# Softmax products for two heads at once, and a spread through DRAM in place of a matmul, in a hybrid decoder layer

## The chip, the core and the metric

The kernel runs on one core of a Trainium2 chip. The metric is the device time of one execution in microseconds. A core has five engines that each work through a queue of their own in order: TensorE (PE in the profile; its weight loads stand apart as PEld), VectorE (DVE), ScalarE (ACT), GpSimd (POOL) and SyncE (SP), which issues the DMA transfers. They meet through semaphores: an instruction waits for what it needs, and all behind it on its engine wait too.

## What is computed

One decoder layer for a sequence of 512 tokens of width 1024, in float32. A combined input projection feeds two mixers side by side, sparse attention (8 heads of 64) and gated DeltaNet (4 heads of 128); their outputs are projected, gated and merged, then normalised; a gated MLP with a short convolution follows, and a second normalisation. Cut to what the change touches:

```python
def reference(x, ...):
    ...
    y_a = nsa_attention(...) @ w_nsa_out        # three branches: compressed, selected, sliding window
    y_b = gated_deltanet(...) @ w_gdn_out
    mix = (sigmoid(gate_a) * y_a + sigmoid(gate_b) * y_b) @ w_o
    x = layer_norm(ALPHA * x + mix, ...)
    return layer_norm(ALPHA * x + conv_ffn(x, ...), ...)

# in nsa_attention, for the selected (s) and the window (w) branch, causal:
    p = softmax(where(dist >= 0, q @ k.T * scale - slope * dist, NEG))
    o = g[1] * (p_s @ v_s) + g[2] * (p_w @ v_w) + g[0] * o_cmp

# in gated_deltanet, for each chunk of 64 tokens:
    m = where(strict, (k * beta) @ k.T * decay, 0)
    T = triangular_solve(eye + m, eye, lower=True, unit_diagonal=True)

def conv_ffn(x, w_up, conv_w, w_down):
    h = causal_dwconv(x @ w_up, conv_w)
    gate, val = split(h, 2)
    return (silu(gate) * val) @ w_down
```

## The kernel before

A product in float32 precision is made of float32r matmuls: each operand is split into a high part (a copy on ACT, `wh`, `dh`, `pth`) and a low part (a subtraction on DVE or POOL, `wl`, `dl`, `ptl`), and high times high, high times low and low times high are added up in PSUM. Small products are taken in float32 as they are; such a matmul stands in the trace as two records.

The work has stages. The **first stage** (about 324 us) holds the input projection (31 of its 40 units of 128 columns, tile `pg`, three raw weight buffers `raw`), both mixers, and their small chains. Its order is written by hand: the code of each step (`q0`, `k0`, `i0`, `n0`, ...) is recorded by `draw`, engine by engine, and the table `GIVEN` then issues single instructions in one long list (`n0V` is the next DVE instruction of step `n0`). `PLACE` says which buffer each tile takes. Then come the merge (`pm`, `px`), the output projection (`pw`), the FFN's up products (`pu`, 22 units of two halves) and its down products (`pdna`, `pdnb`), which use a 2x2 block scheme with seven products: sums of blocks (`s1` to `s4`) are formed on DVE while the up products run. In those later stages a scheduler orders the instructions by the order of the code.

Three places matter here. **`gdn_tri`** (step `n`, one for each of the 4 DeltaNet heads) inverts the triangular matrix from diagonal blocks of 16 rows upwards. `f16` holds each row's 16 entries within its diagonal block, (128 rows, 4, 16). For the substitution each row needs the rows of its whole block, `lx`; to spread them, `f16` is multiplied with a mask and a matmul with `same` (ones where two rows share a block) sums over the partitions, in two parts of 512 and 256 columns, which ACT copies to `lx`. Then 15 pairs of small DVE operations follow (`ts<-lx,ts` and `ts<-ts,ts`), and products that join the blocks.

**`scores` and `flip`** (steps `s` and `f`, by head and unit) make the softmax of one or two blocks of 128 query rows, transpose it on PE, and split it into `pth` and `ptl`. After every second flip the products with the values (`vcat`) add into `po`, one bank for one head at a time; a causal block of two query tiles is multiplied whole, with a quarter that is zero:

```python
for br, _ in parts:
    for k in range(4 if t > 1 else 2):
        ...
        for i, src in enumerate((pth, ptl)):
            PE.matmul(o, w, src[:, br, b:b + 2, :], start=(u == 1 and k == 0 and i == 0), stop=False)
```

**The FFN loop** forms, at each odd unit, the sums `s1`, `s2` (with its split `hs`, `ls`) and `s4` for its block, in the profile `s<-fth`, `s<-s,fth`, `ls<-s,hs` and `s<-fth,s`; behind the first down product six adds (`x<-x,pdna`) empty its two banks, ahead of the second product `s2`.

Of the kernel before, what the change touches and what calls it, by code (L numbers as in the profile page):

```python
# [33 lines left out]
          ("same", 128), ("low", 128), ("m16", 128),  # L34
# [9 lines left out]
def shape_consts():  # L44
# [8 lines left out]
    c["same"] = p // 16 == j // 16  # L53
# [16 lines left out]
def layout(a):  # L70
# [18 lines left out]
    for i in range(8):  # L89
# [35 lines left out]
DRAWN = "q0 k0 i0 q1 j0 m0 c n0 i1 v0 j1 p0 v1 a0 o0 b0 y0 a1 b1 m1 n1 i2 j2 a2 b2 o1 y1 m2 v2 q2 a3 n2 b3 o2 y2 q3 p1 g0 k1 a4 i3 j3 b4 g1 m3 a5 n3 b5 a6 v3 g2 o3 b6 g3 a7 g4 b7 y3 g5 g6".split()  # L125
GIVEN = """
t0S@2 t0S@1 t0V@2 t0A@1 t0P@6 t0V@3 t0P@7 t0V@1 t0P@8 t0P@9 t0P@10 t0S t0A t0P@3 t0P@4 t0P@11 t0V t0P*3 t0S*2 t0V*2
t0A t0V t0P t0P@15 t0P@16 t0P@21 t0P*4 t2S t2A t0P@22 t0P@23 t2S t2A t0P*3 t2P@6 t2V*2 t2S t2A@3 t2A t2V t2P@3 t2P@9
t2P t2P@10 t2P@11 t2P*6 t2P@18 t2P@15 t2P@21 t2P@19 t2P@22 t2P*2 t2V t2P t2P@20 t2P@23 t2P*2 t4S@1 t4A@2 t4V@2 t4S
t4A@1 t4V@1 t4A t4P@9 t4P@10 t4V t4P t4P@3 t4P*2 t4S t4A t4P@11 t4P@6 t4P@7 t4P@21 t4P@8 t4P@22 t4P t4P@12 t4P@13 t4V  # L130
t4P@18 t4P t4P@15 t4P@16 t4P@17 t4P@19 t4P@20 t4P*2 t6S t6A t6S*2 t6A@2 t6A t6P@9 t6P@3 t6P@6 t6P t6V@2 t6V@1 t6P@10
t6P@7 t6V t6A t6P@4 t6P t6P@11 t6V t6P@8 t6P@18 t6P@5 t6P@19 t6P@20 t6P*5 t6P@21 t6P*4 w20S uA@8 w20A w20V w20A uA@2
uA@11 cV@8 cV@10 uA@5 w20V zS@6 dV@2 q0P*12 dV@3 dA*2 dV@4 dV@5 dV@6 dV@7 dV@8 dV@9 dV@1 dV@10 dV@11 q0P*12 w18S
w18A@1 w18V@1 uA@6 uV@2 zS@2 w21S w18A w18V k0P*15 dV@12 dV@13 dV@14 dV@15 k0P*2 uA@4 uA@7 uA@3 uA w0S q0A@2 q0A*2
dV@16 k0P*4 dV@17 dV@18 w0A zV@1 k0P q0V@2 q0V@1 q0V k0P w16S w0A w0V@1 w0V k0P k0V*4 dV@19 cS@1 i0P*13 zS@5 w21A w21V
dV@20 k0A*2 w1S uA@9 cV i0P*4 w1G i0P*3 s01P k0V*2 s01P i0P*3 s00P i0P q1P w21A q1P*12 s00P uV w1V i0V*2 dV@21 dV@22
w21V i0V zS s01V s01A q1P*8 uV@3 q1P*3 uA@10 zS i0V i0A zV w17S w1G dV@23 w1V dV@24 uV s04P*2 q1A uA j0P uV dA j0P*3
dV@25 dV@26 dV@27 dV j0P*12 w16A q1A@2 w16G q1A q1V@1 q1V@2 w16A w16G j0P*5 w4S j0P*3 q1V j0A w17A m0G j0V cP*19 i0G
cP m0P j0V*2 cS@3 m1V m0G m0P m0A cS i0G cP*4 dP w17V i0P dP i0P w4V w4V@2 dP i0P w4V*2 cA dA i0P j0A j0V i0A cS i0A
i1P*12 i0A*2 i0V@9 i0V cA*3 s01V m0P*4 n0V@2 m0P@8 i1P s00V s00A cP*2 m0V@1 dV m0P w17A w17V i0G s00V*2 i0V i1P i0V  # L140
m0P m0V s02P m0V m0P cP m0V@4 n0G i0V@8 m1G m0V@5 s04V*2 m0V i1P w2S n0V cP*21 cA*4 cV n0V w2V*2 n0P i1P w2V n0G n0P
w2V n0A i1P*4 n0A n0V s01V i1P*2 n0V*14 w5S i1P*2 cP*15 i1A i1V n0V*2 i0V n0V*2 f00P*2 j0P*3 f00P zS n0V j0P n0V*2
s04A@1 i1V w5A w5V n0V j0A*4 cP cV*2 i1V cA n1V@3 cA f00A s02P s02V s02A cV*3 i1A n0V*2 w7S v0P*18 n0V zS n0V v0P s03P
v0P s04A i1V n0V*2 s03P n0V*2 w5A s03V w3S cA cV w5V j1P v0P*4 v0A*2 j1P*10 cV n0P*2 s02V n0P*6 n0V n0A cP*3 cA*2
cA@15 f00V n0P*4 v0V n0V p0P*4 n0P@18 n0P@19 v0G j0V n0P@20 n0P@21 n0P@22 n0P@23 n0P@24 n0P@25 cV n0A@4 n0V@37 n0P*4
p0P n0A n0V p0P v0V p0P*2 s03A w6S w6A p0V*2 n0P*8 j1P*2 cA@16 cV n0A j1P*8 n0V p0V v0A j1P*2 cA@17 j1P s04V v1P w6A
j1A n0P@38 n0P@39 n0P@40 n0P@41 n0P*3 n0A@7 n0P f01P*3 n0A f01P s03V w3A v0V p0A@1 p0A*2 v0P*2 m3G v0P*2 w6V f01A j0G
v0A s04V cV n0P cA s03V cA y0V@1 n0P*3 n0V v1P*10 v0A*3 j1V*3 cA cV w6V p0A f01V s12P*2 s12V o0P w3A o0A w3G@1 i1P
i1A@6 i1P*3 i1A v1P*2 i1A v1P o0P s04V v1P w3G v1P*3 i1A s10P*2 s10V i1A s11P s12A cA f01P cV cA f01P i1A j1A v1P*3
# [96 lines left out]
def body(ctx: ExitStack, tc: tile.TileContext, d, out):  # L246
# [719 lines left out]
    def flip(h, u, s):  # L966
# [26 lines left out]
        if u < 5:  # L993
            return
# [443 lines left out]
```

## Time and profile before

| | us |
|---|---|
| median of 3 runs | 820.7 (820.41 to 820.8) |
| profiled execution | 821.42 |
| its span, first to last instruction | 819.6 |
| PE busy | 808.5 |
| DVE busy | 638.2 |
| ACT busy | 400.9 |
| POOL busy | 147.6 |

The span is the time between the first and the last instruction on the core; the profiled execution's own time is 1.8 us longer. Busy time counts an instruction from start to end; matmuls overlap, so PE's busy time tells that it always had work, not that it worked at its peak. Rows of groups have the line, engine, operation, out<-in by tile names, shapes and count, then the busy time in us and the mean duration of one in ns, then the idle time ahead of them. L1044 is the loop that issues the hand-written order, L261 the call that all recorded operations of the later stages pass through, so tile names tell more than lines. Rows of waits have who waited, for whom, the total in us, how often, and the longest. Timeline rows have the start and the duration in us. DMA rows have the number of transfers, the size of each, and the median time from issue to landing.

### The profile page before, as it was taken

The numbers are of one execution on the slowest core, as the hardware profiler recorded it, in microseconds if no ns is written. First come the engines' busy times: TensorE is split into PE (matmuls) and PEld (weight loads), VectorE is DVE, ScalarE is ACT, GpSimd is POOL, SyncE is SP. The second block draws the span as 40 slices with busy tenths as digits, with TensorE's granted clock in tenths as the row PEclk, the third lists the DMA queues.
The fourth block names the chain that finished last, engine by engine and source line by source line (L and its number), as shares of the span: only waits on it lengthen the run. The fifth ranks groups of instructions, "written<-read, shape, count | busy, mean of one in ns | idle before, by whom it ended". The sixth has DMA issues, their size and how long they took to land.

```text
span 819.6 us, 12072 instructions
## 1 busy us (share of the span) xinstructions
PE 808.5 (99%) x4244; PEld 684.8 (84%) x4244; DVE 638.2 (78%) x1379; ACT 400.9 (49%) x915; POOL 147.6 (18%) x127
## 2 busy tenths in 40 slices
PE   9999999999999999999999999999999999999996
PEld 9888888888888888887888897888888888878885
DVE  5979888887788777675467548878898889898767
ACT  5444665666776674534342023444444444566530
POOL 0031314232244401212300002111111011100001
PEclk9999999999999999999999999999999999999998
DMA  7432211111120201354463207555556655676922
GB/s 239 128 120 83 63 41 52 52 53 52 33 72 27 78 26 53 116 166 134 149 232 103 77 10 233 191 192 179 184 196 204 206 205 182 187 235 196 339 82 102
DMA packets 40252, 108.06 MB, mean 132 GB/s; under 512 B 4608, under 2 KB 5760, under 8 KB 39936
## 3 DMA queue, kind: packets, MB, share of 16 engines
q1 hardware_dynamic: 40192, 107.30, 39.7%
q8 instruction: 33, 0.54, 0.3%
q14 instruction: 27, 0.22, 0.1%
HBM read 93.65 MB, written 13.63 MB: 131 GB/s over the span
## 4 chain that ended last, share of the span: by engine, by line
PE 85%; DVE 6%; DMA 3%; ACT 2%; issue 2%; POOL 1%; SPq 0%; DVEq 0%; ACTq 0%; POOLq 0%
PE pu L261 25%; PE pg L1044 20%; PE pd L1044 8%; PE pa L1044 6%; PE pdna L261 5%; PE pdnb L261 5%; PE pm L261 5%; PE pw L261 3%; PE px L261 3%; PE po L1044 3%; PE pg L261 2%; DVE fa L261 1%; DVE x L261 1%; DVE wl L261 1%; DMA raw<-tdn 1%
## 5 line engine op out<-in xcount | busy, mean ns | idle before, releaser
L261 PE MATMUL pu<-mh,wl 128*128 128x512 f32 (+1 forms) x384 | 142.7, 372 | 0.7 <-DVE wl L261 0.7
L261 PE MATMUL pu<-mh,wh 128*128 128x512 f32 (+1 forms) x384 | 142.7, 372 | 0.0
L261 PE MATMUL pu<-ml,wh 128*128 128x512 f32 (+1 forms) x384 | 142.6, 371 | 0.0
L261 ACT ACTIVATE wh<-raw 128x512 fp32r<-128x512 f32 (+1 forms) x112 | 71.7, 643 | 80.7 <-PE pu L261 54.0
L261 DVE TENSOR_TENSOR wl<-raw,wh 128x512 fp32r<-128x512 f32 (+1 forms) x108 | 87.7, 817 | 25.6 <-ACT wh L261 21.6
L1044 PE MATMUL pg<-xh,wl 128*128 128x512 f32 x248 | 99.0, 402 | 0.0
L1044 PE MATMUL pg<-xl,wh 128*128 128x512 f32 x248 | 98.9, 400 | 0.0
L1044 PE MATMUL pg<-xh,wh 128*128 128x512 f32 x248 | 97.4, 399 | 0.0
L261 PEld LDWEIGHTS pu<-mh,wl 128*128 128x128 f32 x384 | 72.3, 188 | 13.6 <-DVE wl L261 1.2
L261 PEld LDWEIGHTS pu<-ml,wh 128*128 128x128 f32 x384 | 72.3, 188 | 12.6
L261 PEld LDWEIGHTS pu<-mh,wh 128*128 128x128 f32 x384 | 72.3, 188 | 12.4
L261 DVE SCALAR_TENSOR_TENSOR fa<-pu,fcw,fa 128x511 f32<-128x511 f32 x88 | 65.6, 746 | 10.0 <-ACT fa L261 8.6
L261 POOL TENSOR_TENSOR fth<-fth,fa 128x512 f32<-128x512 f32 x22 | 32.6, 1483 | 211.5 <-DVE fa L261 194.0
L1044 ACT ACTIVATE big<-big,mn 128x256 f32<-128x256 f32 (+3 forms) x84 | 46.0, 553 | 23.9 <-DVE mn L1044 22.2
L1044 POOL TENSOR_TENSOR wl<-raw,wh 128x512 fp32r<-128x512 f32 x28 | 36.6, 1313 | 99.7 <-ACT wh L1044 58.9
L1044 PEld LDWEIGHTS pg<-xh,wl 128*128 128x128 f32 x248 | 46.6, 188 | 9.5 <-issue 0.5
L1044 PEld LDWEIGHTS pg<-xl,wh 128*128 128x128 f32 x248 | 46.6, 188 | 9.0 <-issue 0.2
L1044 PEld LDWEIGHTS pg<-xh,wh 128*128 128x128 f32 x248 | 46.7, 188 | 8.7 <-issue 0.7
L261 ACT ACTIVATE dh<-raw 128x512 fp32r<-128x512 f32 x62 | 36.9, 624 | 23.9 <-DMA raw<-tdn 9.9
L261 DVE TENSOR_TENSOR dl<-raw,dh 128x512 fp32r<-128x512 f32 x62 | 41.1, 695 | 8.9 <-ACT dh L261 8.7
L1044 ACT ACTIVATE wh<-raw 128x512 fp32r<-128x512 f32 (+1 forms) x54 | 32.5, 607 | 9.1 <-PE pg L1044 5.0
L261 POOL TENSOR_TENSOR rs<-rs,minus_half 128x1 f32<-128x1 f32 x8 | 7.5, 942 | 163.2 <-DVE rs L261 163.2
(318 smaller groups left out, 1868.2 us busy)
## 6 DMA issues: line engine op xcount, KB each, us to landing
raw<-in_up SPq DMA_DIRECT2D x44, 512.0 KB, 4.0
raw<-in_wT SPq DMA_DIRECT2D x40, 512.0 KB, 3.5
traw<-in_down SPq DMA_DIRECT2D x22, 512.0 KB, 5.2
tdn<-traw SPq DMA_DIRECT2D x44, 256.0 KB, 2.7
raw<-tdn SPq DMA_DIRECT2D x20, 512.0 KB, 4.4
raw<-in_down SPq DMA_DIRECT2D x15, 512.0 KB, 4.0
raw<-in_wm SPq DMA_DIRECT2D x8, 512.0 KB, 3.6
raw<-in_wo SPq DMA_DIRECT2D x8, 512.0 KB, 3.5
```

The costliest lines, as they stand in the source:

```text
L261: return give(*a, **kw)
L1044: give(*a, **kw)
```

## The change

`gdn_tri` no longer uses `same`. `f16` is written to DRAM sixteen times by one DMA, and a second DMA reads, for each partition, the sixteen rows of its block from its own copy into `lx`, whose layout is now (16, 4, 16). The two masked multiplications, the two matmuls and the two copies of each head go.

```diff
+    f16d = tc.dram_tile([GH, 16, 128 * TT * 16], F32, name="f16d")
...
-        lx = R["lx"].tile((128, TT, 16, 16))
-        for r0, n in ((8, 16), (0, 8)):
-            rs = slice(r0, r0 + 8)
-            sh = (128, TT, 8, n)
-            gx = R["big"].tile(sh)
-            E(f"gx{n}", h).tensor_tensor(gx, bc(f16[:, :, None, :n], sh), bc(C["row"][:, None, rs, None], sh), op=OP.mult)
-            pl = dps(sh)
-            PE.matmul(pl, C["same"], gx, start=True, stop=True)
-            copy(E(f"lx{n}", h, "A"), lx[:, :, rs, :n], pl)
+        lx = R["lx"].tile((128, 16, TT, 16))
+        d = f16d[h]
+        SP.dma_start(out=bass.AP(tensor=f16d.tensor, offset=d.offset, ap=[[64, 128], [8192, 16], [1, 64]]),
+                     in_=bc(f16.rearrange("p c j -> p (c j)")[:, None, :], (128, 16, 64)))
+        SP.dma_start(out=lx.rearrange("p r c j -> p (r c j)"),
+                     in_=bass.AP(tensor=f16d.tensor, offset=d.offset, ap=[[1024, 8], [8192, 16], [1, 1024]]))
...
-            V.tensor_tensor(tmp[:, :, :n], lx[:, :, r + 1:, r], bc(xs[:, :, r:r + 1], (128, TT, n)), op=OP.mult)
+            V.tensor_tensor(tmp[:, :, :n], lx[:, r + 1:, :, r].rearrange("p r c -> p c r"),
+                            bc(xs[:, :, r:r + 1], (128, TT, n)), op=OP.mult)
```

In `flip`, the transposed softmax of two heads of a pair goes into one tile pair `pt` (high and low), and one matmul takes both heads. The block on the diagonal (`k == t`) is multiplied only where it is not zero. `po` now holds one half of the queries for two heads. Units are drawn for both heads of a pair, two at a time.

```diff
-        if t % 2 == 0:
+        pr, hh, e = h // 2, h % 2, u // 2
+        if (pr, e) not in PT:
+            PT[pr, e] = [R["pt"].tile((128, 2, 2, 4, 128), F32R) for _ in range(2)]
...
+        if t % 2 == 0 or hh == 0:
             return
...
+        split = [x.rearrange("p h b k c -> p h (b k c)") for x in PT.pop((pr, e))]
         for br, _ in parts:
-            for k in range(4 if t > 1 else 2):
...
+            for k in range(t + 1):
                 w = vcat[:, k, br, g].rearrange("p a b -> p (a b)")
-                for i, src in enumerate((pth, ptl)):
-                    PE.matmul(o, w, src[:, br, b:b + 2, :], start=(u == 1 and k == 0 and i == 0), stop=False)
+                a, z = (128 if k == t else 0), 256 * k + (0 if late else 512 * br)
+                for i, src in enumerate(split):
+                    PE.matmul(pout[:, :, a:], w, src[:, :, z + a:z + 256],
+                              start=(e != 1 and br == 0 and k == 0 and i == 0), stop=False)
...
         for i in range(2):
-            PE.matmul(pout, vcb[:, g, j].rearrange("p a b -> p (a b)"), PC[g][i], start=False, stop=(i == 1))
+            for n, pc in enumerate(PC[g]):
+                PE.matmul(pout[:, i], vcb[:, g, (h - 1 + i) % 4].rearrange("p a b -> p (a b)"), pc[:, ts],
+                          start=False, stop=(i == n == 1))
```

On PE, before, one such group in the middle of the first stage (`po` is the output bank, `pc` the compressed branch's probabilities; one pth and one ptl row of four equal pairs are shown with what follows):

```order
L1044 MATMUL po_182<-pth,vcat 128x256
L1044 MATMUL po_182<-ptl,vcat 128x256
L1044 MATMUL po_182<-pc_154,vcb 128x512
L1044 MATMUL pd_178<-sq_120,big_87 128x128
L1044 MATMUL pd_177<-kq_118 128x256
L1044 MATMUL po_182<-pc_155,vcb 128x512
```

And after, the end of a group for the later query tiles of two heads (`pg` is the input projection, which stands between):

```order
L1042 MATMUL po_184<-pt_156,vcat 128x512
L1042 MATMUL po_184<-pt_157,vcat 128x512
L1042 MATMUL po_184<-pt_156,vcat 128x2x128
L1042 MATMUL po_184<-pt_157,vcat 128x2x128
L1042 MATMUL pg_186<-xh,wl_166 128x512
L1042 MATMUL pg_186<-xh,wh_161 128x512
L1042 MATMUL po_184<-pc_154,vcb 128x256
L1042 MATMUL po_184<-pc_155,vcb 128x256
```

Products with the values now have 512 columns, or twice 128 on the diagonal; those with `vcb` have 256 and are twice as many. In the whole program 192 + 16 `po` matmuls become 96 + 32.

The first stage's order (`GIVEN`, `DRAWN`, `PLACE`) is drawn anew, so nearly all its rows move. A line or two of the table:

```diff
-t0A t0V t0P t0P@15 t0P@16 t0P@21 t0P*4 t2S t2A t0P@22 t0P@23 t2S t2A t0P*3 t2P@6 t2V*2 t2S t2A@3 t2A t2V t2P@3 t2P@9
...
+BUFS = {'big': 23, 'rnd': 7, 'kq': 2, 'lx': 1, 'sq': 7, 'ts': 6, 'row': 16, 'mn': 3, 'k': 2, 'pc': 2, 'pt': 2, 'raw': 3, 'wh': 3, 'wl': 3, 'pg': 2, 'pd': 2, 'pa': 3, 'po': 1, 'mg': 6, 'mr': 4, 'dw': 7}
```

On DVE, before, from the reduce that makes `f16` of the first head (`ts_128`) to the first use of `lx`:

```order
L1044 TENSOR_REDUCE ts_128<-big_109 128x64
L1044 COPY kv<-pos 128x8x4
L1044 TENSOR_TENSOR big_89<-ts_128,cst 128x512
L1044 CAST wh_159<-raw_156 128x512
L1044 TENSOR_TENSOR wl_162<-raw_156,wh_159 128x512
L1044 CAST wh_160<-raw_156 128x512
L1044 TENSOR_TENSOR wl_164<-raw_156,wh_160 128x512
L1044 TENSOR_TENSOR ts_129<-lx_119,ts_127 128x4x15
```

After, the same stretch; the middle rows of the sixteen in between are left out here:

```order
L1042 TENSOR_REDUCE ts_128<-big_88 128x64
L1042 ISA big_89,mn_149<-pa_182,cst 128x384
L1042 ISA mn_149 128x1
L1042 CAST wh_163<-raw_159 128x512
L1042 TENSOR_TENSOR wl_164<-raw_159,wh_163 128x512
...
L1042 SCALAR_TENSOR_TENSOR big_91<-pg_186,gcw,big_91 128x511
L1042 SCALAR_TENSOR_TENSOR big_91<-pg_186,gcw,big_91 128x510
L1042 SCALAR_TENSOR_TENSOR big_91<-pg_186,gcw,big_91 128x509
L1042 TENSOR_TENSOR big_87<-pd_179,big_107 128x256
L1042 TENSOR_TENSOR ts_129<-lx_119,ts_127 128x4x15
```

Six rows stood between the two before, sixteen do now; for the other three heads there are now 23, 28 and 26. On SyncE the write and the read of `lx` stand next to each other, at the third head with one weight load between them.

In the FFN loop, `s2` and `s4` of a block are formed one unit later, behind the conv of the next unit's second half, and the six adds behind the first down product are spread over the steps of the second:

```diff
+    def second_sums(b, even, odd, after=None):
+        s2 = fs.tile([128, 256], F32, name="s2", bufs=1)
+        x = E("s2", b).tensor_tensor(s2, SUM["s1"][:, b], even, op=OP.subtract)
+        if after and E("s2", b) is V:
+            later(x, after)
+        halves("s2", b, s2)
+        E("s4", b).tensor_tensor(SUM["s4"][:, b], odd, s2, op=OP.subtract)
+
     for p in range(NF):
         g = []
         for b in range(2):
+            if b and p and p % 2 == 0:
+                second_sums(*held, turn)
...
-    for i in range(2):
-        add(i, n2, pa_[i], True)
-        add(2 + i, n1, pa_[i], True)
-        add(2 + i, n2, pa_[i], True)
+
+    def spread():
+        for i in range(2):
+            for t, cs in ((i, n2), (2 + i, n1), (2 + i, n2)):
+                yield add(t, cs, pa_[i], True)
+
+    work.append(spread())
     mul("s2", tdn[1], pb_)
+    work.clear()
```

On DVE at the FFN's third unit, before (`fa` is a conv tap, `wl` a weight's low part):

```order
L261 TENSOR_TENSOR s_4564<-s_4508,fth 128x256
L261 SCALAR_TENSOR_TENSOR fa_4599<-pu_4574,fcw,fa_4599 128x510
L261 TENSOR_TENSOR ls_4504<-s_4564,hs_4503 128x256
L261 TENSOR_TENSOR s_4510<-fth,s_4564 128x256
L261 TENSOR_TENSOR wl_164<-raw_157,wh_161 128x512
```

and after:

```order
L257 TENSOR_TENSOR wl_166<-raw_158,wh_161 128x512
L257 SCALAR_TENSOR_TENSOR fa_4505<-pu_4480,fcw,fa_4505 128x510
L257 TENSOR_TENSOR s_4509<-s_4421,fth 128x256
L257 TENSOR_TENSOR wl_164<-raw_158,wh_162 128x512
L257 TENSOR_TENSOR ls_4417<-s_4509,hs_4416 128x256
```

The first `wl` moved from behind the sums to ahead of them.

More of the change, by code (lines that the diff above doesn't have):

```diff
@@ L33 @@
 CONSTS = [("ident", 128), ("upper", 128), ("after", 128), ("ones", 128),
-          ("same", 128), ("low", 128), ("m16", 128),
+          ("low", 128), ("m16", 128),
           ("alibi", 512), ("cbias", 128), ("blk", 8), ("row", 16), ("seen", 4), ("slope", 8)]
@@ L133 @@
[L133 to L137, printed above, removed]
@@ L233 @@
+    'wl': '0120120120121021021002212012020210202012011220010212102012102121021102012',
+    'rnd': '1034526562016253',
     'k': '0101',
     'kq': '0101',
-    'row': '0123579abf486cde1805437296cb',
-    'ts': '102431024153',
+    'row': '01238567a349bcdef08c194562bd',
+    'ts': '102531045123',
     'lx': '0000',
     'pc': '0101',
-    'mn': '101022210102120012122110122021010012001012012120',
+    'sq': '01234562612356412063512540443126525043142650312340543126',
+    'mn': '201101102002121220120120211012022100120100122021',
@@ L348, in body @@
     R = {n: Places(sp.tile, n, BUFS[n], size) for n, size in (
-        ("big", 512), ("rnd", 512), ("kq", 1024), ("lx", 1024), ("sq", 128), ("ts", 64), ("row", 16), ("mn", 8), ("k", 1024), ("pc", 512))}
+        ("big", 512), ("rnd", 512), ("kq", 1024), ("lx", 1024), ("sq", 128), ("ts", 64), ("row", 16), ("mn", 8), ("k", 1024), ("pc", 512), ("pt", 2048))}
     R.update({n: Places(wp.tile, n, BUFS[n], size) for n, size in (("raw", 1024), ("wh", 512), ("wl", 512))})
@@ L925, in cmp_attn @@
         PC[g] = (hi, lo)
-    pth = nsa.tile([128, 2, 8, 128], F32R, name="pth")
-    ptl = nsa.tile([128, 2, 8, 128], F32R, name="ptl")
-    for t in (pth, ptl):
-        G.memset(t[:, :, 6, :].bitcast(F32), 0.0)
     UNITS = [((0, 2),), ((0, 3),), ((1, 2),), ((1, 3),), ((0, 0), (1, 0)), ((0, 1), (1, 1))]
-    POUT, SC = {}, []
+    PT, POUT, SC = {}, {}, []
     def scores(h, u):
@@ L975, in flip @@
                 PE.transpose(pt[:, i, k, :], s[:, i, k * 128:(k + 1) * 128], ident)
-        first = t - 2 if t > 1 else 4 + t
-        own = (slice(br, br + len(parts)), slice(first, first + 2 * t + 1, 2))
-        th, tl = pth[:, own[0], own[1], :], ptl[:, own[0], own[1], :]
+        pr, hh, e = h // 2, h % 2, u // 2
+        if (pr, e) not in PT:
+            PT[pr, e] = [R["pt"].tile((128, 2, 2, 4, 128), F32R) for _ in range(2)]
+        view = (lambda x: x[:, hh, :, t:3 * t + 1:2, :]) if t < 2 else (
+            lambda x: x[:, hh].rearrange("p b k c -> p (b k) c")[:, None, t - 2:3 * t - 1:2, :])
@@ L979, in flip @@
+        th, tl = (view(x) for x in PT[pr, e])
         A.activation(th, pt, AF.Copy)
         V.tensor_tensor(tl, pt, th.bitcast(F32), op=OP.subtract)
-        if t % 2 == 0:
+        if t % 2 == 0 or hh == 0:
             return
-        if u == 1:
-            POUT[h] = R["po"].tile()
-        pout = POUT[h]
+        late = t > 1
+        if e != 1:
+            POUT[late] = R["po"].tile((128, 2, 256))
+        pout = POUT[late]
+        split = [x.rearrange("p h b k c -> p h (b k c)") for x in PT.pop((pr, e))]
@@ L994, in flip @@
+        if e == 0:
             return
-        j = h % 4
+        ts = slice(256, 512) if late else slice(0, 256)
         for i in range(2):
-            PE.matmul(pout, vcb[:, g, j].rearrange("p a b -> p (a b)"), PC[g][i], start=False, stop=(i == 1))
-        ob = R["big"].tile()
-        copy(E("ob", h, "A"), ob[0:64], pout[64:128])
-        r0 = 64 * (h % 2)
-        if h % 2 == 0:
-            oT[h // 2] = yo_tile("oT")
-        V.tensor_tensor(oT[h // 2][r0:r0 + 64], pout[0:64], ob[0:64], op=OP.add)
@@ L1004, in flip @@
-        Q2.pop(h)
+            for n, pc in enumerate(PC[g]):
+                PE.matmul(pout[:, i], vcb[:, g, (h - 1 + i) % 4].rearrange("p a b -> p (a b)"), pc[:, ts],
+                          start=False, stop=(i == n == 1))
+        ob = R["big"].tile((128, 2, 256))
+        copy(E("ob", 2 * pr + late, "A"), ob[0:64], pout[64:128])
+        if late:
+            oT[pr] = yo_tile("oT")
+        for i in range(2):
+            V.tensor_tensor(oT[pr][64 * i:64 * i + 64, ts], pout[0:64, i], ob[0:64, i], op=OP.add)
@@ L1029, in body @@
             continue
-        for u in (0, 1, 2) if name[0] == "a" else (3, 4, 5):
-            draw(f"s{at[0]}{u}", lambda: SC.append((at[0], u, scores(at[0], u))))
-            for x in SC[:] if u == 5 else SC[:-LAG]:
+        pr, e = divmod(at[0], 3)
+        for h, u in itertools.product((2 * pr, 2 * pr + 1), (2 * e, 2 * e + 1)):
+            draw(f"s{h}{u}", lambda: SC.append((h, u, scores(h, u))))
+            for x in SC[:] if h % 2 and u % 2 else SC[:-LAG]:
                 draw(f"f{x[0]}{x[1]}", flip, *SC.pop(0))
@@ L1206, in body, with later @@
     tr = pool(tq, name="tr", bufs=1, side="left")
+    def later(x, y):
+        tc.add_manual_dep(x.ins, y.ins.name, mybir.DependencyInfo(
+            mybir.DependencyClass.NoSync, mybir.DependencyReason.SCHED_ONLY), reason="not before its turn")
     def weight_sums(b, after):
@@ L1215, in weight_sums @@
         if e is V:
-            tc.add_manual_dep(one.ins, after.ins.name, mybir.DependencyInfo(
-                mybir.DependencyClass.NoSync, mybir.DependencyReason.SCHED_ONLY), reason="not before its turn")
+            later(one, after)
         e.tensor_tensor(b12, b22, b12, op=OP.subtract)
@@ L1244, in body @@
                 n = 2 - i
[L1245 to L1246 removed]
+                turn = V.scalar_tensor_tensor(acc[:, n:], ps[:, :S - n], w[:, i:i + 1], acc[:, n:],
+                                              op0=OP.mult, op1=OP.add)
             g.append(acc)
@@ L1341, in body @@
     mul("11", dn[:, 0, :, 0, :], pa_, early={0: wp, 2: tl})
-    for i in range(2):
-        add(i, n2, pa_[i], True)
-        add(2 + i, n1, pa_[i], True)
-        add(2 + i, n2, pa_[i], True)
+    def spread():
+        for i in range(2):
+            for t, cs in ((i, n2), (2 + i, n1), (2 + i, n2)):
+                yield add(t, cs, pa_[i], True)
+    work.append(spread())
     mul("s2", tdn[1], pb_)
+    work.clear()
     for i in range(2):
```

197 lines of the change are left out of this document (94 added, 103 removed).

## Prediction

> **What bounds the kernel now.** I read the page first, then who waited for whom on TensorE, then the busy time by stretches, and last the timeline at the places that the change touches.
>
> ```profile
> span 819.6 us, 12072 instructions
> PE 808.5 (99%) x4244; PEld 684.8 (84%) x4244; DVE 638.2 (78%) x1379; ACT 400.9 (49%) x915; POOL 147.6 (18%) x127
> ```
>
> TensorE (PE) is busy for 99% of the span, and the next engine, VectorE (DVE), for 78%. A busy PE need not be a fast one, so the second question is how often it stood still:
>
> ```profile
> PE pu L261 <- DVE wl L261: 0.7, 1, 0.7
> PE pd L1044 <- ACT big L1044: 0.7, 1, 0.7
> PE pdnb L261 <- DVE dl L261: 0.5, 1, 0.5
> PE pd L1044 <- DVE big L1044: 0.3, 1, 0.3
> ```
>
> These are four of the eight waits of PE in the whole run; none is over 1.0 us. In the first stage (L1044, up to about 324 us) PE waited for DVE once, 0.3 us, and for ScalarE (ACT) once, 0.7 us. The kernel is bound by the number of columns that PE streams, stage by stage, so an edit is worth what it takes out of PE's queue, less what it makes PE wait.
>
> ```profile
> 50.00:300.00 250.00, 248.90 (x1577) 213.99 (x1576) 206.32 (x637) 158.34 (x468) 73.44 (x65) 1.00 0.17 54
> ```
>
> This is the busy time in the middle of the first stage (PE, weight loads, DVE, ACT, POOL, then granted clock, DMA share, GB/s). The clock is full. DVE has 206.3 of 250 us: 17.5% of its time is free, and one DVE row takes 250 / 637 = 0.39 us of time on average.
>
> **What PE pays per instruction.** A matmul's own duration holds its latency, since matmuls are pipelined; the price is the distance from start to start.
>
> ```profile
> 250.03 0.39 PE L1044 MATMUL pg<-xh,wh 128*128 128x512 f32 x1
> ...
> 251.18 0.39 PE L1044 MATMUL pg<-xh,wl 128*128 128x512 f32 x1
> ...
> 251.64 0.28 PE L1044 MATMUL po<-ptl,vcat 128*128 128x256 f32 x1
> ...
> 252.35 0.28 PE L1044 MATMUL po<-ptl,vcat 128*128 128x256 f32 x1
> ...
> 256.37 0.60 PE L1044 MATMUL pd<-big,cst 128*128 128x256 f32 x2
> 256.62 0.58 PE L1044 MATMUL pg<-xl,wh 128*128 128x512 f32 x1
> 257.03 0.39 PE L1044 MATMUL pg<-xh,wl 128*128 128x512 f32 x1
> ...
> 260.09 1.02 PE L1044 MATMUL pd<-big,cst 128*128 128x512 f32 x2
> 260.56 0.79 PE L1044 MATMUL pg<-xh,wl 128*128 128x512 f32 x1
> 261.19 0.40 PE L1044 MATMUL pg<-xh,wh 128*128 128x512 f32 x1
> ```
>
> Five steps of 512 columns lie between the first two rows: 1.15 / 5 = 0.23 us each. Six steps of 256 columns lie between the next two: 0.71 / 6 = 0.118 us. The products with `same` are float32 (not float32r) and stand as two records each. The matmul behind them begins late: from 260.09 to 261.19 are 1.10 us, of which one step of 0.23 belongs to the pg matmul, so the 512-column product costs 0.87 us; from 256.37 to 257.03, 0.66 - 0.23 = 0.43 us for the 256-column one. Their records alone (below) would give less.
>
> ```profile
> L1044 PE MATMUL po<-pth,vcat 128*128 128x256 f32 x96 | 25.5, 289 | 0.0
> L1044 PE MATMUL po<-ptl,vcat 128*128 128x256 f32 x96 | 24.8, 283 | 0.0
> L1044 PE MATMUL po<-pc,vcb 128*128 128x512 f32 x16 | 5.5, 407 | 0.0
> L1044 PE MATMUL pd<-big,cst 128*128 128x512 f32 x8 | 4.1, 593 | 0.0
> L1044 PE MATMUL pd<-big,cst 128*128 128x256 f32 x8 | 2.4, 379 | 0.0
> ```
>
> **The change, part by part.**
>
> *The `same` products go.* Eight records are four products of each size: 4 x (0.87 + 0.43) = **5.2 us** off PE. They lie between other matmuls with no wait, so all of it counts. Their inputs (DVE, POOL) and the eight `lx` copies (ACT) go too, from engines that are not the bound: nothing.
>
> *Softmax products for two heads.* Before: 192 x 0.118 + 16 x 0.23 = 26.3 us. After, by the program's order: 64 of 512 columns with vcat, 32 of 2x128 with vcat, 32 of 256 with vcb: 64 x 0.118 + 64 x 0.23 = 22.3 us. That is **4.1 us** off PE (the zero quarter of each causal block is no longer multiplied, and there are 80 fewer instructions). The new tile pair `pt` is used whole by each group of four flips, so the next group's copies on ACT and DVE wait for the last po matmul of the one before; at the tightest place some 40 PE rows lie between two groups, against 4 copies on each engine, and I cost this at nothing. The output adds are 16 of 64x256 instead of 8 of 64x512, on DVE's free time.
>
> *The FFN's second sums come later.* PE stood still once at the third unit:
>
> ```profile
> 499.14 0.39 PE L261 MATMUL pu<-ml,wh 128*128 128x512 f32 x1
> 500.26 0.50 PE L261 MATMUL pu<-mh,wl 128*128 128x512 f32 x1 [0.73 <-DVE wl L261]
> ```
>
> ```profile
> 497.86 0.41 DVE L261 TENSOR_TENSOR s<-s,fth 128x256 f32<-128x256 f32 x1
> 498.20 0.74 DVE L261 SCALAR_TENSOR_TENSOR fa<-pu,fcw,fa 128x510 f32<-128x510 f32 x1
> 498.86 0.41 DVE L261 TENSOR_TENSOR ls<-s,hs 128x256 fp32r<-128x256 f32 x1
> 499.19 0.42 DVE L261 TENSOR_TENSOR s<-fth,s 128x256 f32<-128x256 f32 x1
> 499.52 0.68 DVE L261 TENSOR_TENSOR wl<-raw,wh 128x512 fp32r<-128x512 f32 x1
> ```
>
> The step was 1.12 instead of 0.23 us. The new order puts this wl directly behind the first fa: it would end at about 497.9 + 0.7 = 498.6, before PE needs it. The next wl moves up with it. **0.9 us** gained; ends 0 and 0.9.
>
> *The adds behind the first down product are spread.* PE's other stop there is
>
> ```profile
> 727.06 0.39 PE L261 MATMUL pdnb<-dh,hs 128*128 128x512 f32 x1
> 728.00 0.50 PE L261 MATMUL pdnb<-dl,hs 128*128 128x512 f32 x1 [0.55 <-DVE dl L261]
> ```
>
> ```profile
> 723.67 3.67 DVE L261 SCALAR_TENSOR_TENSOR x<-x,pdna 128x512 f32<-128x512 f32 x6
> 727.26 3.09 DVE L261 TENSOR_TENSOR dl<-raw,dh 128x512 fp32r<-128x512 f32 x5
> ```
>
> Six adds stood ahead of the dl that PE needed. With one add for two dl, DVE has 2 x 0.62 + 0.61 = 1.9 us of work for each 12 matmuls, 2.7 us of PE. 0.94 - 0.23 = **0.7 us** gained; ends 0 and 0.7.
>
> *The DRAM round trip is the new wait.* `f16` is written sixteen times (512 KB in 2048 pieces of 256 bytes); when that has landed, SyncE issues the read of `lx` (512 KB, 128 pieces of 4 KB); the first of DVE's 30 steps waits for it, and all DVE work behind, weight splits (`wl`) included, waits too. No row shows such a write. The nearest:
>
> ```profile
> raw<-in_wT SPq DMA_DIRECT2D x40, 512.0 KB, 3.5
> tdn<-traw SPq DMA_DIRECT2D x44, 256.0 KB, 2.7
> ln<-in_lnr SPq DMA_DIRECT2D x2, 1024.0 KB, 6.1
> out_dram<-x SPq DMA_DIRECT2D x2, 128.0 KB, 2.0
> ```
>
> If time goes by bytes, the write lands in 3.5 us (first row). If it goes by pieces: tdn has 128 pieces and 0.7 us over the 2.0 of the smallest store; 16 times as many give 2.0 + 16 x 0.7 = 13.2 us. I take 5, nearer to the first: half the bytes in as many pieces (out_dram, tdn) change the store by 0.7 us, so pieces are not the whole price. The read is raw<-in_wT's form, 3.5 us; its upper end is 6.1, a transfer of twice the bytes. With 0.4 us for each of two issues, the trip c is 0.4 + 5 + 0.4 + 3.5 = 9.3 us; ends 7.8 and 20.1.
>
> What covers it is the DVE work between the reduce that makes `f16` and the first use of `lx`: 16, 23, 28 and 26 rows in the four heads by the new order, at 0.39 us 6.3, 9.0, 11.0 and 10.2 us. Of a late DVE I let 17.5% of c be absorbed by its free time; the rest goes to PE: 0.825 x 9.3 - 6.3 = 1.4 us at the first head, nothing at the others. **+1.4 us**; ends -0.3 (the old chain's own wait, below, which PE felt at most as its 0.3 us) and, at c = 20.1, 10.3 + 7.6 + 5.6 + 6.4 = 29.9.
>
> ```profile
> DVE ts L1044 <- ACT lx L1044: 2.5, 2, 2.0
> ```
>
> SyncE's queue stands still behind the read as well. Weight loads wait there for up to c, but three `raw` buffers are ahead of them; nothing.
>
> *The order of the first stage, drawn anew.* All engines' rows there move. PE has little to win (1.0 us of waits); what it loses shows in no row. I take 0, and hold -1.0 to +4.6 open (rivals).
>
> Sum: -5.2 - 4.1 - 0.9 - 0.7 + 1.4 = -9.5 us. The profiled execution took 821.4 us (span 819.6 and 1.8 around it), so 811.9; the median of the runs is 0.7 us lower: **811.2 us**.
>
> [...]
>
> **The rivals.**
> 1. *Both legs cost like twice their bytes* (6.1 us each, the 1024 KB row): c = 13.0, PE loses 4.4 + 1.7 + 0.5 = 6.6 us: 820.7 - 10.9 + 6.6 = 816.4. [...] Against: stores of 128 and 256 KB land within 0.7 us of each other. 13%.
> 2. *Slower: the trip goes by pieces*, c = 20.1, and DVE stands at all four heads: 820.7 - 10.9 + 29.9 = 839.7. It decides from c = 14.4, where 4 x 0.825 x 14.4 - 36.5 = 10.9. 6%.
> 3. *PE was not alone*: DVE is over 80% busy in this stage, and PE's freed 9.3 us come back half as waits for copies and splits (+4.6): 815.8. Against: PE waited 1.0 us in all there. 9%.
> 4. *The new order also ends the stage's waits* (0.7 and 0.3 us) and the trip is covered: 820.7 - 10.9 - 1.0 = 808.8. 10%.
> 5. *Nothing happens*: terms cancel within 0.2% (1.6 us, about what a measurement of this kernel can tell from no change). 3%.
>
> **How the numbers follow.** The forecast has 59%, with 809 to 814 as its own range. Rivals 1 and 3 reach up to 818 and rival 4 down to 807; leaving out rivals 2 and 5 and the edges, the range is 807.0 to 817.5. Faster by over 0.2% are the forecast and rivals 1, 3, 4: 0.91; within 0.2%, 0.03; slower, 0.06.
>
> **What would show it.** No pd<-big,cst group and 128 po matmuls; PE steps of 0.23 and 0.118 us in the po groups; no wait at the third unit's wl nor at the first dl of the s2 product; f16d<-ts landing in about 5 us and lx<-f16d in 3.5; DVE waiting for lx at the first head alone. A write over 8 us, or PE waits of several us in the first stage, would make the sum wrong.

## The result, and the profile after

| | before | after |
|---|---|---|
| median of 6 runs each | 820.7 us (819.8 to 821.0) | 814.7 us (814.4 to 815.5) |
| ratio, 95% interval | | 0.9927 (0.9916 to 0.9937) |
| first pg matmul of the profiled run | 18.53 | 19.43 |
| first px matmul (end of the first stage) | 324.16 | 319.43 |
| first pu, first pdna matmul | 464.11, 706.66 | 459.18, 700.70 |
| start of the last matmul, span | 812.34, 819.6 | 805.53, 812.8 |

The change gained 6.0 us; 9.5 were forecast. The last four rows are starts read from the two timelines (the first pg matmul is that of the input projection). They say where: the FFN gave what was forecast (below), and the first stage, from its first pg matmul to the first px, fell from 305.63 to 300.00 us, by 5.6 where 5.2 + 4.1 - 1.4 = 7.9 were forecast.

The head of the page and who waited for whom on PE, after the change (four of its nine rows):

```profile
span 812.8 us, 11878 instructions
PE 800.5 (98%) x4148; PEld 675.7 (83%) x4148; DVE 629.6 (77%) x1383; ACT 395.1 (49%) x907; POOL 141.7 (17%) x121
```

```profile
PE pd L1042 <- DVE sq L1042: 0.9, 1, 0.9
PE pd L1042 <- DVE wh L1042: 0.8, 1, 0.8
PE pd L1042 <- DVE big L1042: 0.7, 1, 0.7
PE pg L1042 <- DVE wl L1042: 0.5, 1, 0.5
```

The waits of the third unit's wl and of the first dl are gone. In their place PE waits for DVE in the first stage, at the products pd and pg. Only the first of these rows lies at a trip (below); the others lie at 7.9, 318.7 and 31.5 us. The new product groups, by shape:

```profile
L1042 PE MATMUL po<-pt,vcat 128*128 128x512 f32 x64 | 18.5, 396 | 0.3 <-DVE pt L1042 0.3
L1042 PE MATMUL po<-pt,vcat 128*128 128x256 f32 x32 | 7.1, 279 | 0.0
L1042 PE MATMUL po<-pc,vcb 128*128 128x256 f32 x32 | 6.9, 296 | 0.0
```

64 + 32 + 32 = 128, as counted from the order, and no pd<-big,cst is left. From the start of one such row to the next start on PE are 0.227 us for the first group and 0.117 for the second (medians), the steps that were forecast. The round trip, from the issues (count, KB each, median us to landing) and from the view of the tile lx:

```profile
f16d<-ts SPq DMA_DIRECT2D x4, 512.0 KB, 3.6
lx<-f16d SPq DMA_DIRECT2D x4, 512.0 KB
```

```profile
L1042 SPq DMA_DIRECT2D lx<-f16d x4: 604/611/723, 69.0 to 247.9; - x4
its engine sat idle before it (us, times) until:
  DMA lx<-f16d: 5.7, 3
```

The write lands in 3.6 us, sooner than the 5 I took. For the read the profile gives no landing; DVE's waits for it bound it. At the fourth head (DVE, then PE):

```profile
253.37 0.08 DVE L1042 DVE_READ_ACCUMULATOR2_ANT mn<- 128x1 f32 x1
256.39 0.26 DVE L1042 TENSOR_TENSOR ts<-lx,ts 128x60 f32<-128x60 f32 x1 [2.94 <-DMA lx<-f16d]
...
257.20 0.68 DVE L1042 TENSOR_TENSOR pt<-pa,pt 128x512 fp32r<-128x512 f32 x1
...
260.62 0.33 DVE L1042 SCALAR_TENSOR_TENSOR sq<-sq,eg,pd 128x128 f32<-128x128 f32 x1
```

```profile
257.29 0.39 PE L1042 MATMUL po<-pt,vcat 128*128 128x512 f32 x1
257.94 1.68 PE L1042 MATMUL po<-pt,vcat 128*128 128x512 f32 x7 [0.26 <-DVE pt L1042]
259.45 0.60 PE L1042 MATMUL pa<-ident,big 128*128 128x128 f32 x4
261.00 0.49 PE L1042 MATMUL pd<-sq,kq 128*128 128x128 f32 x2 [0.95 <-DVE sq L1042]
```

Read it downwards: DVE has nothing left at 253.4, lx comes at 256.4, the copies `pt` and `sq` behind it are late, and PE stands twice. The write was issued at 244.57 and the read at 247.89, so the read took about 8.5 us from its issue, and the trip 11.8; at the first head it is 65.68 to 76.79, 11.1 us. The prediction had 9.3, and let only the first head lose. DVE stood for lx for 2.3 us at the first head, not at all at the second, 0.5 at the third and 2.9 at the fourth.

### The profile page after: what moved, and what is told of

The parts are those of the page before. It is cut to its first block, busy times and chain, and to the rows that moved or that the text cites. A ratio compares the mean times of both kernels' runs of the same rounds, so it can differ in the third digit from the quotient of the medians.

```text
span 812.8 us, 11878 instructions
## 1 busy us (share of the span) xinstructions
PE 800.5 (98%) x4148; PEld 675.7 (83%) x4148; DVE 629.6 (77%) x1383; ACT 395.1 (49%) x907; POOL 141.7 (17%) x121
## 4 chain that ended last, share of the span: by engine, by line
PE 84%; DVE 7%; DMA 5%; ACT 1%; issue 1%; POOL 1%; SPq 0%; DVEq 0%; ACTq 0%; POOLq 0%
PE pu L257 30%; PE pg L1042 13%; PE pdna L257 7%; PE pd L1042 6%; PE pdnb L257 6%; PE pw L257 5%; PE pm L257 5%; PE pa L1042 5%; DMA lx<-f16d 3%; PE pg L257 2%; DVE ts L1042 2%; PE px L257 2%; PE po L1042 2%; DVE big L1042 2%; DMA f16d<-ts 1%
## 5 line engine op out<-in xcount | busy, mean ns | idle before, releaser
L1042 ACT ACTIVATE big<-big,mn 128x512 f32<-128x512 f32 (+3 forms) x84 | 46.2, 555 | 21.0 <-DVE mn L1042 20.5
L1042 PEld LDWEIGHTS pg<-xh,wl 128*128 128x128 f32 x248 | 46.6, 188 | 10.2 <-DVE wl L1042 1.2
L257 DVE TENSOR_TENSOR dl<-raw,dh 128x512 fp32r<-128x512 f32 x62 | 41.4, 698 | 10.2 <-ACT dh L257 10.1
```

What stands on the lines that cost most here:

```text
L257: return give(*a, **kw)
L1042: give(*a, **kw)
```

## Theories

A: the trip is the loss; its read is slow since it runs on 8 of 16 engines (its DMA share of 0.49 is shown below). B: the read is slow for another reason (its freshly written copies, its bytes). C: the loss is the order drawn anew, whose waits at 31.5, 55.6 and 318.7 us have no lx near.

## Experiments on the round trip

The edits are shown shortened: `AP` stands for `bass.AP`, a tensor for its view or its offset, and in long lists most entries are left out.

**Two copies, read from 16 blocks.**

```diff
-SP.dma_start(out=AP(f16d, ap=[[64, 128], [8192, 16], [1, 64]]), in_=bc(f16, (128, 16, 64)))
-SP.dma_start(out=lx, in_=AP(f16d, ap=[[1024, 8], [8192, 16], [1, 1024]]))
+for i in range(2):
+    SP.dma_start(out=AP(f16d, offset + 1024 * i, ap=[[2048, 8], [64, 16], [1, 64]]), in_=f16)
+SP.dma_start(out=lx, in_=AP(f16d, ap=[[1024, 16], [0, 8], [1, 1024]]))
```

> The changed kernel, but f16 is written twice (two writes of 32 KB) instead of sixteen times, laid out so that the read of lx has 16 blocks as its slowest dimension instead of 8; the read itself stays 512 KB in 4 KB pieces. Theory A (the read is slow because it runs on 8 of 16 engines, and DVE's waits for it cost PE about 0.4 us at the first head and 1.5 us at the fourth): the trip falls from 11-12 us to about 7, DVE does not wait for lx any more, and the time falls by about 1.9 us to 812.8. Theory B (the read is slow for another reason, so its 7 us stay; only the write gets shorter): the trip falls to 9.5 us, the fourth head's wait falls from 2.9 to about 1, time 813.8. Theory C (the missing 3.5 us lie in the new order, not in the trip): 814.4 to 815.

**One copy, read from 8 blocks.**

```diff
-SP.dma_start(out=AP(f16d, ap=[[64, 128], [8192, 16], [1, 64]]), in_=bc(f16, (128, 16, 64)))
-SP.dma_start(out=lx, in_=AP(f16d, ap=[[1024, 8], [8192, 16], [1, 1024]]))
+SP.dma_start(out=AP(f16d, ap=[[64, 128], [1, 64]]), in_=f16)
+SP.dma_start(out=lx, in_=AP(f16d, ap=[[1024, 8], [0, 16], [1, 1024]]))
```

> The changed kernel, but f16 is written once (32 KB, 128 pieces of 256 B), and the read of lx repeats it sixteen times with a stride of zero; its slowest dimension stays 8. Theory A (8 engines): the write lands in about 2 us, the read still takes 7 us, DVE still waits at the fourth head, but 1.5 us less; time about 814. Theory B (the read is slow because its pieces come from sixteen freshly written copies, or for the bytes of the write beside it): the read takes 3.5 us, no DVE wait, 812.8. Theory C (order): 814.4 to 815.

**A read that waits for nothing.**

```diff
-SP.dma_start(out=lx, in_=AP(f16d, ap=[[1024, 8], [8192, 16], [1, 1024]]))
+SP.dma_start(out=lx, in_=AP(in_wo, ap=[[1024, 8], [8192, 16], [1, 1024]]))   # issued some 250 instructions earlier
```

> The changed kernel, but lx is read from a weight matrix, some 250 instructions ahead of where f16 is written, so that nothing waits for the round trip; the write, its bytes and the read's bytes stay. lx does not hold the products of this head, so the substitution is left out in effect. Theory A (trip): DVE's 5.7 us of waits for lx go, and with them about 1.9 us of PE: 812.8. Theory C (order): 814.4 to 815. Either way this is the floor for what any faster trip can bring in this order.

**The changed kernel once more**, for comparison, and to see its start again.

> The changed kernel itself, on the chip of the next three, to compare them with and to see whether its late start (first pg matmul at 19.43 us instead of 18.53) is the kernel's or that execution's. If the start is its order's doing: again about 19.4. If it is how the first loads happened to land (three variants with the same first 18 us of order began at 18.7 to 18.9): about 18.8. Ratio to before 0.9927 again.

| kernel | median us | ratio to before (95%) | first pg to first px | DVE's waits for lx |
|---|---|---|---|---|
| after | 814.7 | 0.9927 (0.9916 to 0.9937) | 300.00 | 5.7 us, 3 times |
| after, again | 814.5 | 0.9920 (0.9907 to 0.9932) | 300.89 | 7.0 us, 4 times |
| two copies, 16 blocks | 811.4 | 0.9877 (0.9861 to 0.9892) | 297.00 | none |
| one copy, 8 blocks | 810.9 | 0.9871 (0.9858 to 0.9885) | 297.05 | 1.2 us, 2 times |
| read not waiting | 810.7 | 0.9869 (0.9856 to 0.9883) | 296.93 | none |

Each ratio is to the kernel before as measured beside that run (820.7 to 821.4 us); the last two columns are of one profiled execution each.

Theory A holds, and with more than its 1.9 us: without the wait the stage is 3.1 us shorter than in the first profile of after, and 4.0 shorter than in the second. The changed kernel and the one that does not wait have the same matmuls in the same order, so their starts can be compared row by row. The lag of the first profile grows by 0.6 us at the first head, 0.0 at the second, 0.6 at the third and 1.8 at the fourth (3.0 in all); of the second by 0.4, 0.5, 1.1 and 1.9 (3.9). The fourth head's rows of the kernel that does not wait show no stop where the changed one stood twice:

```profile
255.40 1.75 PE L1126 MATMUL po<-pt,vcat 128*128 128x512 f32 x8
256.99 0.60 PE L1126 MATMUL pa<-ident,big 128*128 128x128 f32 x4
257.43 0.39 PE L1126 MATMUL pd<-sq,kq 128*128 128x128 f32 x2
```

Why the read is slow is told by the first two experiments. The issues of the one with two copies:

```profile
lx<-f16d SPq DMA_DIRECT2D x4, 512.0 KB, 4.4
```

and of the one with one copy:

```profile
f16d<-ts SPq DMA_DIRECT2D x4, 32.0 KB, 1.4
```

Both have few, fresh copies. With 16 blocks the read lands in 4.4 us (the one landing that the profile has, at the fourth head). With 8 it is issued at 66.44 and DVE, waiting, starts at 74.18:

```profile
66.44 0.72 SPq L1042 DMA_DIRECT2D lx<-f16d  x1
74.18 0.26 DVE L1042 TENSOR_TENSOR ts<-lx,ts 128x60 f32<-128x60 f32 x1 [0.38 <-DMA lx<-f16d]
```

These are 7.7 us, as in the changed kernel (68.99 to 76.79: 7.8); at the fourth head it is 8.2 (244.28 to 252.52). There two weight loads are issued behind the read in both variants, so they do not make the difference. So neither the sixteen copies nor the bytes make it slow; the 8 blocks do, and theory B falls. The packets of the stretch from 69 to 78 us, in which one read of lx and one weight load ran, say the same (the changed kernel first, then two copies, then one copy):

```profile
DMA packets 281, 1.07 MB, mean 118 GB/s; under 512 B 24, under 2 KB 24, under 8 KB 280
```

```profile
DMA packets 289, 1.07 MB, mean 118 GB/s; under 512 B 32, under 2 KB 32, under 8 KB 288
```

```profile
DMA packets 244, 0.91 MB, mean 102 GB/s; under 512 B 24, under 2 KB 24, under 8 KB 243
```

A weight load by itself has 16 packets under 512 B (the kernel before, 75 to 80 us), so of these counts the read has 24 - 16 = 8 with 8 blocks and 32 - 16 = 16 with 16. How many of the 16 DMA engines are busy shows in the changed kernel at the third head, first while the read of lx runs alone, then while a weight load does (length, busy time of PE, PEld, DVE, ACT and POOL, granted clock, DMA share, GB/s):

```profile
180.00:181.50 1.50, 1.50 (x9) 1.28 (x8) 1.13 (x4) 1.48 (x6) 0.60 (x1) 1.00 0.49 161
186.50:187.50 1.00, 1.00 (x6) 0.81 (x5) 0.89 (x5) 1.00 (x4) 0.00 (x0) 1.00 0.98 389
```

Of 16 engines, a share of 0.49 amounts to 8 and a share of 0.98 to all.

## Experiments on the order

**The first 18 us in the order of before** (only rows of the recorded order are exchanged).

```diff
-t0S t0A t0S t0V@2 t0P@3 t0V@3 t0V t0P@4 t0P@5 t0S t0S@4 ...
+t0S@2 t0S@1 t0V@2 t0A@1 t0P@6 t0V@3 t0P@7 t0V@1 t0P@8 ...
```

> The changed kernel with the first 18 us (the four t steps, all engines and their loads) in the order of before. Theory C (the new order costs at its start: first pg matmul at 19.43 instead of 18.53): about 0.9 us faster, 813.8. Theory A (only the trip costs): no change, 814.4 to 815.

816.7 us, ratio 0.9938 (0.9926 to 0.9951): not faster, and its first pg matmul at 19.41, with the start of before. The changed kernel's second profile began at 18.90, its variants that have the same start of their order between 18.41 and 19.18. So the 0.9 us by which after's first profile began later belongs to the execution, not to the order.

**Three places mended.**

```diff
-dV@17 q0V@1 q0A q0V zS@4 k0P*8 w0A w0V@1 w0V i0P
+dV@17 q0V@1 w0A q0A w0V@1 w0V q0V zS@4 k0P*8 i0P
-j0V m0G m0P*2 j0V*2 w4V j0A
+j0V m0G m0P*2 j0V w4V j0V j0A
-ENGINE = {
+ENGINE = {'ws31': 'V',
```

> The changed kernel with the round trip as it is and three pieces of its order mended where PE stood without any lx wait near: two wl splits moved ahead of a rnd row (PE stood 0.70 us at 31.5), one wh cast moved ahead of a convolution row (0.50 us at 55.6), and the wl splits of weight tile 31 moved from POOL to DVE so that they do not stand before a rsqrt (0.85 us at 318.7). Theory C (the new order costs 2.0 us by these three): 2.0 us faster than the changed kernel on the same chip, ratio about 0.990. If DVE's queue just passes the delay on: under 0.5 us faster.

> The one-copy round trip together with the three mended places. The two are at different places, so they should add: the changed kernel less 4 us (one copy: ratio 0.987) less 2 us (mended places): ratio about 0.9845, some 808.6 us where before takes 821.3. If DVE as such is the limit (PE not alone), the sum falls short by a microsecond or more.

The mended order alone gives 813.6 us, ratio 0.9911 (0.9897 to 0.9925): its interval overlaps the changed kernel's, so 0.9 us of gain is not told from none. With the one-copy trip it gives 810.1, ratio **0.9864** (0.9851 to 0.9878), the fastest version here and clearly faster than both kernels, though not told apart from one copy alone (0.9871). It is 1.5 us short of the 808.6 expected, since the three places gave 1.1 us and not 2.0. Row by row against one copy alone, one mend worked: the stop at the end of the stage (0.87 us) is gone. The first only moved its wait to the next matmul, now for the `rnd` row that it had pushed back:

```profile
29.88 0.50 PE L1042 MATMUL pg<-xh,wh 128*128 128x512 f32 x1 [0.41 <-DVE rnd L1042]
```

That lost 0.57 where 0.69 were won. The second took its stop from 0.50 only to 0.37. Theory C is worth about one microsecond in these places, not two.

## Experiments on the kernel before

**The FFN edits alone** (the whole of the diff from `later` on, and nothing ahead of it).

```diff
+            if b and p and p % 2 == 0:
+                second_sums(*held, turn)
...
+    work.append(spread())
     mul("s2", tdn[1], pb_)
```

> The kernel before with only the two FFN edits (second sums one unit later, adds spread over the next product). By the two stalls that they end, 0.9 and 0.7 us: 1.6 us faster, ratio 0.9980. If the stalls only move: no change.

819.1 us, ratio 0.9971 (0.9958 to 0.9983), so 1.4 to 3.4 us. Its FFN runs from the first pu to the first pdna in 241.52 us (before: 242.55) and from there to the last matmul in 104.83 (105.68): 1.0 + 0.9 = 1.9 us. After's profile has the same two lengths.

**Without the `same` products, nothing waiting.**

```diff
-gx = R["big"].tile(sh)
-E(f"gx{n}", h).tensor_tensor(gx, ...)
-PE.matmul(pl, C["same"], gx, start=True, stop=True)
-copy(E(f"lx{n}", h, "A"), lx[:, :, rs, :n], pl)
+SP.dma_start(out=AP(f16d, ap=[[64, 128], [8192, 16], [1, 64]]), in_=bc(f16, (128, 16, 64)))
+SP.dma_start(out=lx, in_=AP(in_wo, ap=[[1024, 8], [8192, 16], [1, 1024]]))
```

> The kernel before, in its own order and with its own softmax, without the products with `same`, their inputs and the copies behind them; f16 is written sixteen times as in the changed kernel and lx is read, well ahead, from a weight matrix, so that nothing waits for the trip (the substitution is left out in effect). If the products cost PE what the distances in the profile said (4 x (0.87 + 0.43) = 5.2 us): 816.1 where before takes 821.3, ratio 0.9937. If they cost only their records' busy time (4.1 + 2.4 = 6.5 us): 0.992. If they lay beside PE's waits: 0.997 or more.

818.9 us, ratio 0.9969 (0.9956 to 0.9981). The total is that of the last account, the rows are the first's: matched one by one with those of before, PE's rows gain 1.3 us at each of the four heads, 5.2 in all, so the price was right. But the stage is only 1.8 us shorter (303.82 against 305.63): 2.8 us are given back between the second and the third head and 0.6 behind the fourth. The largest piece is one new wait:

```profile
PE pa L1130 <- DVE ptl L1130: 1.5, 1, 1.5
```

DVE and POOL ahead of it:

```profile
144.34 0.23 DVE L1130 TENSOR_TENSOR ts<-lx,ts 128x44 f32<-128x44 f32 x1
144.60 1.16 DVE L1130 TENSOR_TENSOR ts<-ts,ts 128x44 f32<-128x44 f32 x1
...
147.12 1.02 DVE L1130 TENSOR_TENSOR ptl<-pa,pth 128x256 fp32r<-128x256 f32 x2
```

```profile
144.37 1.33 POOL L1130 TENSOR_TENSOR wl<-raw,wh 128x512 fp32r<-128x512 f32 x1 [2.66 <-issue]
```

A DVE row of 0.2 us lasted 1.16, until POOL's split ended, and the `ptl` that PE needed stood behind it; that is some 1.0 of the 1.5 us. With the work shifted, an order drawn for other times puts rows side by side that hinder each other.

**The DMA spread in before's order, waiting.**

```diff
+SP.dma_start(out=lx, in_=AP(f16d, ap=[[1024, 8], [8192, 16], [1, 1024]]))
```

(In place of the read from the weight matrix; both transfers right behind the reduce.)

> The kernel before with the DMA spread alone, as the changed kernel has it (sixteen copies, read on 8 blocks), in the order of before: the write and the read stand right behind the reduce, and 5, 10, 10 and 17 DVE rows lie between the reduce and the first use of lx, instead of 16, 23, 28 and 26. With the trip at 11.1 us as measured in the changed kernel and 0.39 us a row, DVE waits 9.1 + 7.2 + 7.2 + 4.5 = 28 us; at the share that PE felt in the changed kernel (3.1 of 5.7 us) PE loses 15 us: 821 - 5 + 15 = 831. By the prediction's own rule (0.825 c less the rows): 836. If the new order was not needed for the trip (DVE catches up): 817 to 821.

852.3 us, ratio 1.0376 (1.0362 to 1.0391): slower than before by 31 us, slower by 33 than the same kernel with nothing waiting, and worse than each account. Its longest waits, PE's and then DVE's for lx:

```profile
PE pa L1129 <- DVE big L1129: 7.5, 1, 7.5
PE po L1129 <- ACT pth L1129: 6.8, 1, 6.8
PE pg L1129 <- ACT wh L1129: 4.9, 1, 4.9
PE pa L1129 <- DVE mn L1129: 4.7, 2, 4.2
```

```profile
  DMA lx<-f16d: 15.7, 2
```

PE's long stops, of 4.2 to 7.5 us, lie one at each head. DVE's two waits for lx, of 9.4 and 6.3 us, are at the first and the third head. At the second and the fourth, DVE does not wait for lx at all; there the late one is a weight load, which SyncE issued behind the read of lx (at 148.58 and 281.18 us), and with it ScalarE's copy `wh`:

```profile
156.59 0.63 ACT L1129 ACTIVATE wh<-raw 128x512 fp32r<-128x512 f32 x1 [12.27 <-DMA raw<-in_wT]
289.48 0.63 ACT L1129 ACTIVATE wh<-raw 128x512 fp32r<-128x512 f32 x1 [7.13 <-DMA raw<-in_wT]
```

Nor are the stops the whole loss. These are the first stage in the kernel with nothing waiting and in this one, and 6.8 us at its fourth head (length, busy time of PE, PEld, DVE, ACT and POOL, granted clock, DMA share, GB/s):

```profile
18.72:322.54 303.82, 300.50 (x1855) 258.13 (x1853) 250.56 (x757) 181.39 (x530) 82.78 (x72) 1.00 0.26 77
19.06:356.09 337.03, 311.56 (x1854) 265.76 (x1853) 250.62 (x757) 181.44 (x530) 82.76 (x72) 0.95 0.25 69
289.34:296.15 6.81, 5.23 (x17) 4.59 (x18) 4.45 (x16) 1.39 (x3) 1.27 (x1) 0.50 0.00 0
```

PE stood still for 22.2 us more, and for the same matmuls it was busy for 11.1 us more. Late in each of the four long stops the granted clock fell to 0.50 and stayed there for 6.8 to 10.2 us, into the matmuls behind the stop, some 31 us in all; a step of 512 columns there took 0.43 us in place of 0.23. In the changed kernel, whose stops in this stage are 1.0 us at most, it stayed at 1.00. In this order, then, a third of what the trip cost was a slower PE behind its stops; how long a stop must be for the clock to fall is not shown.

The order drawn anew is therefore no side matter: in it the same trip costs 3 to 4 us. It puts other DVE work between the write and the first use, and no weight load behind the read comes so late that PE stands.

## Why the prediction was right, and what it mis-sized

The direction and the parts taken off PE were right, and the range holds the result. The forecast itself was off: 814.7 us lies outside the forecast's own 809 to 814, nearer to the third rival (815.8) and the first (816.4) than to 811.2. The range reached it because it was drawn to take those rivals in.

- **The `same` products, 5.2 us.** Right: 5.2 by the four places in before's order. What the records alone would have given (6.5) was too much; the distance from start to start was the right measure.
- **Softmax for two heads, 4.1 us.** Not run alone, since its steps have no place in before's order. Added up from each row's start to the next start on PE, the po rows take 27.7 us in before's trace and 22.8 in that of the kernel that does not wait for lx: 4.9 less. The count times the usual step, which gave 4.1, leaves out the slower steps next to other products. Without the trip's wait the stage is 305.63 - 296.93 = 8.7 us shorter, where 5.2 and 4.1 to 4.9 make 9.3 to 10.1.
- **FFN, 0.9 and 0.7 us.** Right in both, 1.0 and 0.9 by the stage lengths.
- **The round trip, 1.4 us, is the term that was mis-sized**: 3.1 and 4.0 us in two profiles. The trip takes 11.1 to 11.8 us and not 9.3: the write was sooner (3.6 for 5), but the read took about 8 where I gave it 3.9 with its issue, the price of a weight load, whose DMA share is 0.98 where the read's is 0.49. The cover, rows times 0.39 us, was wrong place by place, since an average over 250 us says little about ten of them: at the first head DVE had work until 74.5, 8.8 us after the write and not 6.3; at the fourth until 253.5, 8.9 us and not 10.2. With one copy, where the trip is 9.2 us at the first head (64.99 to 74.18) and 9.7 at the fourth, PE loses 0.1 us (297.05 against 296.93), so the forecast's own 9.3 us would have cost next to nothing. What lies beyond the cover PE feels unevenly: 0.6 of DVE's 2.3 us at the first head, 1.8 of 2.9 at the fourth. That "only the first head loses" was wrong; the fourth lost most. With the measured trip the forecast's rule gives 0.825 x 11.1 - 6.3 = 2.9 us at the first head and nothing at the fourth: near the right total, but by chance.
- **SyncE's queue, nothing.** True in the new order; in before's order two of the four long stops came from weight loads behind the read.
- **The new order, 0.** Not measured by itself. By difference it costs 0.6 to 1.4 us, of which 0.9 at the one place where a mend worked. The waits of the old order that it ended were three and not two, as the prediction has them: a wait of 0.2 us for ScalarE's `xh` at the start belongs to them.
- **The first rival** (both legs like twice their bytes, 816.4) was right for one leg. The read, on 8 engines (DMA share 0.49), took about 8 us, more even than its 6.1. The write of 2048 pieces of 256 bytes did not go by twice its bytes: 3.3 to 3.9 us at the four heads, as long as a weight load of the same size (3.5). **The second** (by pieces, 20 us) fell with that. **The third** (freed time comes back as waits) happened little in the redrawn order, but it did in the old one: 3.4 of 5.2 us.
- Of the 6.9 us between the two profiled spans: -5.2, -4.1, +0.6 (what is left for the order if softmax gave 4.1), +3.1 and -1.9, +0.9 for the later start, and -0.2 between the first px and the first pu, give -6.8.

## What to carry to other kernels

Before a transfer is priced by its bytes, look at the blocks that it reads: 8 as the slowest dimension instead of 16 cost this read 3.3 to 3.8 us, and a second copy in DRAM, or one written copy read sixteen times, made the trip fit. The trip cost next to nothing where the work in front of the wait nearly covered it (with one copy 0.1 us of PE for 9.2 and 9.7 us); price that cover by where the engine really runs dry, not by an average. And in a recorded order an edit and the order belong together: the spread that gains here costs 31 us in the order of before.

## What was not expected of the hardware

Some short DVE rows of the substitution, which began while POOL ran a split, lasted until just behind its end: 1.16 instead of 0.2 us above (to 145.76, POOL's split to 145.70), and in the changed kernel, right behind the fourth head's late lx, 1.29 us beside POOL's 1.28:

```profile
261.79 1.29 DVE L1042 TENSOR_TENSOR ts<-lx,ts 128x28 f32<-128x28 f32 x1
```

```profile
261.77 1.28 POOL L1042 TENSOR_TENSOR wl<-raw,wh 128x512 fp32r<-128x512 f32 x1 [7.02 <-ACT wh L1042]
```

The kernel before has it too, at 199.03 us (0.77 us, to 199.80; the split to 199.76) and at 267.25 us (0.40 us, to 267.65; the split to 267.59). A row that began just ahead of a split, at 270.15 us there (the split at 270.19), took its usual 0.20 us. Why the rows last so long is not shown. With two copies the long row is another, at 251.95 us (1.16 us), and the row of 128x28 goes free: none that reads lx takes over 0.26 us. The other surprise is the store: 512 KB in 2048 pieces of 256 bytes landed as fast (3.6 us) as a weight load of 512 KB in pieces of 4 KB (3.5 us).
